# A hybrid GLA / DeltaNet layer: timed VectorE and ScalarE steps kept in emission order, the modulation's last step as a task, other charges on the planner's clock

## The chip, the cores and the metric

One core of a Trainium2 chip. The time is the device time of one launch, in microseconds (us). The engines are TensorE (PE in the profile; PEld its weight loads), VectorE (DVE), ScalarE (ACT), GpSimd (POOL) and SyncE (SP, which issues most DMAs). In the trace each runs its instructions in the order in which the built program lists them.

## The reference

One layer of a streaming encoder on 512 prompt and 64 sample tokens, width 2048, in float32:

```python
mod = jax.nn.silu(c) @ w_ada[l] + b_ada[l]
sh1, sc1, g1, sh2, sc2, g2 = jnp.split(mod[:, None, :], N_MOD, axis=-1)
h = rmsnorm(x, norm1[l]) * (1 + sc1) + sh1
mix, s_a, s_b, s_c = token_mixers(h, ...)      # w_in, GLA (4 heads) and gated DeltaNet (8 heads), w_out
x = x + g1 * mix
h = rmsnorm(x, norm2[l]) * (1 + sc2) + sh2
f, s_f = conv_ffn(h, ...)                      # w_up, causal conv of width 3, silu(gate) * val, w_down
x = x + g2 * f
```

A DeltaNet head normalizes q and k, forms two 128x128 matrices of decays for each block, solves a triangular system (the inverse of 1 + lower), and carries a state through the blocks. A GLA head does the like with a decay for each channel. `c` is one vector for the prompt and one for the sample.

## The kernel before

**Stages.** `head` (to about 180 us): norm, the first third of the modulation, and the first projections. Then the mixers (`gdn_heads`, `gla_heads`): projection tiles of `w_in`, each 16 steps of six matmuls (`mm6`: activations and weights are each split into a rounded part `h` and a rest `l`, and three of the four products are taken). Between those steps the work of the heads is woven in. Then the output projection's first half (k = 8 to 15), after it the second half (from about 1140 us), whose activations `oa` are loaded from DRAM and rounded by `load_o`; last the FFN (`up`, `down`), the longest stage.

**Weights.** `wtile`/`split` loads 128x1024 weights into a `raw` buffer (three of them), rounds them on ACT into `wh`, and takes the rest on DVE into `wl`.

**Jobs, tasks, ada.** Every PE step calls `tick`. It moves the planner's clock `now` on by 0.795 us and asks three kinds of Python generators for work: tasks (convolutions, gates), jobs (the heads: `gdn`, `gla`) and `ada`, the last two thirds of the modulation. `ada` adds up on DVE, in 512-column steps, `acc += w * c`; one block of 512 outputs takes 64 such steps (`acc` in the profile), and there are 16 blocks. At a block's end `ada_sum` sums over the partitions with PE (L1095), copies to `rows` on ACT, transposes and adds the bias (`put_mod`).

**The clock.** Every instruction that goes through `_Timed` is charged to its engine by `charge`, from `OP_US`: a base and a price for an element, added to the time at which the engine comes free (`free`), or to the job's own chain. A generator yields (`until`, `hop`, `pause`) until `now` has passed the end of what it waits for; only then is its next instruction emitted. So the clock decides between which projection steps a head's matmuls stand.

**Who orders the queues.** After emission the framework's scheduler lists the instructions. It goes by priority, which is the place of emission, and takes the next one whose producers it holds for ready. `high_priority(offset=80)` moves an instruction 80 places ahead. Weights have that (`split`), and so do all DVE and ACT steps of the jobs (`_Sooner`). `issue_after(x)` puts an instruction behind `x` on its engine.

**The inverse.** In `inverse16` a head's matrix goes to DRAM and comes back as 32 small 16x16 blocks, 28 dependent DVE steps invert them (L432 and L433, `m<-m 32x14` and the like), they go out again and come back as `cm`, and two DVE steps (L449) make of them the tiles that PE reads at L263.

In the profile all timed steps have the lines of their helpers: L2248 for `_Timed`, L2224 for the jobs' steps, L2264 for their matmuls, L2260 for transposes, L2278 for POOL. In the changed kernel these are L2272, L2247, L2287, L2283 and L2305.

## Time and profile before

| what | us |
|---|---|
| median of 3 runs (2776.75 to 2779.93) | 2779.32 |
| the profiled execution's own time | 2773.29 |
| its span, first to last instruction | 2771.5 |
| PE busy in the span | 2719.0 |
| DVE busy | 2276.2 |
| ACT busy | 1298.6 |
| POOL busy | 468.7 |

A line of a group reads: line, engine, operation, output <- inputs, shape, count | busy us, mean ns of one | idle time of the engine just before them, and what ended most of it. A line of the waits reads: who waits and at which line, for whom; then us in total, how often, the longest. A line in order of time reads: start, duration, what, and in brackets the idle time before it and its releaser.

### The profile page before, as it was taken

What the parts mean: (1) busy time and instruction counts of PE and PEld (TensorE: products, weight loads), DVE (VectorE), ACT (ScalarE), POOL (GpSimd) and SP (SyncE); (2) the same over time, 40 slices, a digit from 0 to 9 for tenths busy, and PEclk for the clock granted to TensorE, in tenths of its full rate; (3) what the DMA queues carried; (4) which work ended last, traced back from release to release, by engine and by line L of the source; (5) the groups of instructions that cost most, each with busy time, mean ns of one, the idle gap of its engine ahead of it and who ended that gap; (6) DMA issues with size and microseconds to landing.
All of it is one profiled execution on the core that took longest, in us unless ns stands there. A gap on an engine that the chain in (4) does not pass through costs nothing.

```text
span 2771.5 us, 52615 instructions
## 1 busy us (share of the span) xinstructions
PE 2719.0 (98%) x20528; PEld 2651.8 (96%) x20528; DVE 2276.2 (82%) x3682; ACT 1298.6 (47%) x2269; POOL 468.7 (17%) x440
## 2 busy tenths in 40 slices
PE   7999999999999999999999999999999999999998
PEld 5799999999999999999999999999999999999998
DVE  4578787877878887678999999999999976888896
ACT  4255555464544442355454545444444445333453
POOL 0001000010000000000333333333333300000141
PEclk9999999999999999999999999999999999999999
DMA  9985545555545667634555555554646496764752
GB/s 310 339 263 166 139 137 146 148 148 141 172 139 143 178 180 224 179 101 120 152 166 159 173 153 178 153 181 144 182 142 190 139 315 181 223 209 129 238 175 86
DMA packets 647198, 487.59 MB, mean 176 GB/s; under 512 B 66953, under 2 KB 569988, under 8 KB 646948
## 3 DMA queue, kind: packets, MB, share of 16 engines
q1 hardware_dynamic: 633844, 470.74, 56.7%
q10 hardware_dynamic: 13104, 13.47, 1.7%
q8 instruction: 162, 2.65, 0.4%
q14 instruction: 88, 0.72, 0.1%
HBM read 400.08 MB, written 84.04 MB: 175 GB/s over the span
## 4 chain that ended last, share of the span: by engine, by line
PE 81%; DVE 10%; DMA 3%; issue 2%; ACT 2%; POOL 1%; SPq 0%; ACTq 0%; DVEq 0%; POOLq 0%
PE g L651 16%; PE bank L1738 16%; PE bank L1737 16%; PE bank L1739 16%; PE g L653 8%; PE bank L2264 4%; DVE acc L2248 2%; DVE wl L1647 2%; PE bank L651 1%; PE bank L2260 1%; DVE wl L2248 1%; PE bank L878 1%; DVE m L2224 1%; DVE slot L1933 1%; PE bank L653 1%
## 5 line engine op out<-in xcount | busy, mean ns | idle before, releaser
L1738 PE MATMUL bank<-slot,wh 128*128 128x290 f32 (+1 forms) x3584 | 1067.3, 298 | 0.0
L1737 PE MATMUL bank<-slot,wh 128*128 128x290 f32 (+1 forms) x3584 | 1063.2, 297 | 1.1 <-DVE v L1760 0.6
L1739 PE MATMUL bank<-slot,wl 128*128 128x290 f32 (+1 forms) x3584 | 1059.9, 296 | 0.7 <-DVE wl L1647 0.6
L1739 PEld LDWEIGHTS bank<-slot,wl 128*128 128x128 f32 x3584 | 680.0, 190 | 2.3 <-DVE wl L1647 1.9
L1737 PEld LDWEIGHTS bank<-slot,wh 128*128 128x128 f32 x3584 | 675.1, 188 | 5.7 <-issue 4.4
L1738 PEld LDWEIGHTS bank<-slot,wh 128*128 128x128 f32 x3584 | 677.0, 189 | 0.1
L651 PE MATMUL g<-hh,wh 128*128 128x288 f32 x2048 | 469.9, 310 | 0.6 <-ACT wh L1044 0.3
L653 PE MATMUL g<-hh,wl 128*128 128x288 f32 x2048 | 441.6, 296 | 2.9 <-DVE wl L1046 2.3
L1645 ACT ACTIVATE wh<-raw 128x1024 fp32r<-128x1024 f32 (+1 forms) x304 | 280.6, 923 | 347.8 <-PE bank L1738 322.7
L651 PE MATMUL g<-hl,wh 128*128 128x288 f32 x2048 | 442.2, 297 | 0.3 <-DVE hl L682 0.2
L1647 DVE TENSOR_TENSOR wl<-raw,wh 128x1024 fp32r<-128x1024 f32 (+1 forms) x304 | 372.3, 1225 | 69.7 <-ACT wh L1645 67.5
L1645 ACT ACTIVATE wh<-s 128x1024 fp32r<-128x1024 f32 (+1 forms) x228 | 210.9, 927 | 297.4 <-PE bank L1738 138.0
L651 PEld LDWEIGHTS g<-hh,wh 128*128 128x128 f32 x2048 | 324.8, 189 | 16.2 <-issue 10.5
L653 PEld LDWEIGHTS g<-hh,wl 128*128 128x128 f32 x2048 | 330.3, 189 | 5.1 <-DVE wl L1046 2.7
L651 PEld LDWEIGHTS g<-hl,wh 128*128 128x128 f32 x2048 | 330.1, 189 | 3.3 <-issue 2.3
L1647 DVE TENSOR_TENSOR wl<-s,wh 128x1024 fp32r<-128x1024 f32 (+1 forms) x228 | 251.1, 1103 | 14.5 <-ACT wh L1645 13.4
L2248 ACT ACTIVATE wh<-raw 128x1024 fp32r<-128x1024 f32 x135 | 142.8, 1058 | 192.4 <-PE g L651 176.5
L2248 DVE TENSOR_TENSOR wl<-raw,wh 128x1024 fp32r<-128x1024 f32 x135 | 165.7, 1228 | 50.0 <-ACT wh L2248 47.3
L2248 DVE SCALAR_TENSOR_TENSOR acc<-aw,ct,acc 128x512 f32<-128x512 f32 x284 | 201.7, 744 | 1.5 <-DMA aw<-in_w_ada_dram 1.4
L1861 POOL TENSOR_TENSOR j<-j,j 128x288 f32<-128x288 f32 (+1 forms) x120 | 186.1, 1558 | 83.8 <-ACT j L1865 82.1
L2248 DVE SCALAR_TENSOR_TENSOR acc<-xr,ct,acc 128x512 f32<-128x512 f32 x196 | 141.1, 748 | 0.3 <-DVE rq L2224 0.3
L1933 DVE TENSOR_TENSOR slot<-bank,slot 128x288 f32<-128x288 f32 x184 | 83.2, 452 | 33.6 <-PE bank L1739 32.1
(330 smaller groups left out, 3309.3 us busy)
## 6 DMA issues: line engine op xcount, KB each, us to landing
raw<-in_w_up_dram SPq DMA_DIRECT2D x176, 512.0 KB
raw<-in_w_in_dram SPq DMA_DIRECT2D x100, 512.0 KB
raw<-in_w_down_dram SPq DMA_DIRECT2D x128, 320.0 KB
aw<-in_w_ada_dram SPq DMA_DIRECT2D x79, 512.0 KB
slot<-cd SPq DMA_DIRECT2D x140, 288.0 KB
cd<-j SPq DMA_DIRECT2D x120, 288.0 KB
xr<-in_w_ada_dram SPq DMA_DIRECT2D x49, 512.0 KB
hraw<-in_w_ada_dram SPq DMA_DIRECT2D x40, 512.0 KB
```

Source lines behind the costliest of these rows:

```text
L651: T.matmul(ps[:, h if bank is None else bank, :n], wh, x[:, h, :n], start=f, stop=False)
L653: T.matmul(ps[:, h if bank is None else bank, :n], wl, ah[:, h, :n], start=False, stop=stop)
L878: T.matmul(ps[32 * k:32 * k + 32, :w], cs[:, k0 + k], got[n][k // per][:, k % per], start=(n == together - 1 + 8 * g + 4 * (1 - mi)), stop ...
L1645: self.nc.scalar.activation(hi, src, AF.Copy)
L1647: self.nc.vector.tensor_tensor(lo, src, hi.bitcast(F32), op=ALU.subtract)
L1737: T.matmul(ps, wh[:, j], hi, start=(c < 3 and j == 0), stop=False, skip_group_check=True)
L1738: T.matmul(ps, wh[:, j], lo, start=False, stop=False, skip_group_check=True)
L1739: T.matmul(ps, wl[:, j], hi, start=False, stop=(j == n - 1), skip_group_check=True)
L1861: minus = lambda out, a, b: G.tensor_tensor(out, a, b, op=ALU.subtract)
L1933: V.tensor_tensor(dst, ps, dst, op=ALU.add)
L2248: return f(*a, **kw)
L2264: return self.engine.matmul(out, *a, **kw)
```

## The change

It has four parts.

1. `_Timed` keeps, for DVE and for ACT, the last timed instruction and emits the next one with `issue_after` on it. So all timed steps of an engine stand in emission order, the jobs' too. The weight roundings of `split` are exempt (`floating`).
2. `ada_sum` no longer waits for the copy to `rows`: the copy, the transposes and the bias become a task (`ada_put`), and `ada` goes on with its next block. A second `drain` at the stage's end takes what such a task may leave.
3. ACT's charges: 0.09 us and 1/1060 us for an element in place of 0.10 and 1/960; 0.06 instead of 0.2 where a sum is accumulated; 0.06 for a bias or scale by columns; 1.28 where the function's table differs from the last one's (exp, silu, ln). The 2.6 us charged by hand in `gla_gate` go. DVE's steps with a sum lose their 0.2.
4. POOL's power for the norms is charged 1.0 us more than its base in place of 0.7.

```diff
-OP_US = {"V": (0.12, 1 / 960.0), "A": (0.10, 1 / 960.0), "G": (0.45, 1 / 400.0)}
+OP_US = {"V": (0.12, 1 / 960.0), "A": (0.09, 1 / 1060.0), "G": (0.45, 1 / 400.0)}
+TABLE_US, COLUMN_US = 1.28, 0.06
+TABLES = {AF.Exp: "exp", AF.Silu: "silu", AF.Ln: "ln"}
...
-        self.slower("G", 0.7)
+        self.slower("G", 1.0)
...
+    def action(self, func, *a, **kw):
+
+        us = 0.06 if "accum_out" in kw else 0.0
+        if any(isinstance(kw.get(n), bass.AP) for n in ("bias", "scale")):
+            us += COLUMN_US
+        table = TABLES.get(func, self.table)
+        if table != self.table:
+            self.table, us = table, us + TABLE_US
+        return us
+
+    def behind(self, key):
+
+        last = self.last_of.get(key)
+        return nullcontext() if self.floating or last is None else self.tc.issue_after(last)
...
             nc.sync.dma_start(raw[:, :n_].rearrange("p (k n) -> p k n", k=k), src)
+            self.floating = True
             self.ta.activation(hi[:, :n_], raw[:, :n_], AF.Copy)
             self.tv.tensor_tensor(lo[:, :n_], raw[:, :n_], hi[:, :n_].bitcast(F32), op=ALU.subtract)
+            self.floating = False
...
+        self.spawn(self.ada_put(blk, ps))
+
+    def ada_put(self, blk, ps):
         rows = self.sp.tile([P, 256], F32, tag="qc", bufs=3, name=self.name("rows"))
-        _, at = self.timed(self.ta.activation, rows, ps[:, :256], AF.Copy)
-        yield from self.pause(at)
+        self.ta.activation(rows, ps[:, :256], AF.Copy)
+        yield from self.until()
...
                 yield from self.pause(self.free["V"] + HOP_US)
-                yield from self.ada_sum(blk, acc)
+                self.ada_sum(blk, acc)
...
-        self.slower("A", 2.6)
...
-            self.k.charge(self.key, _size(out), 0.2 if "accum_out" in kw else 0.0)
-            return f(*a, **kw)
+            self.k.charge(self.key, _size(out), self.k.action(*a[2:], **kw) if name == "activation" else 0.0)
+            with self.k.behind(self.key):
+                r = f(*a, **kw)
+            if not self.k.floating and self.key in "VA":
+                self.k.last_of[self.key] = self.k.tc.nc.cur_bb.bb.instructions[-1]
+            return r
```

No instruction is added or removed on DVE or PE; four of ACT's table loads go. From the end of `head` to the end of the first half of the output projection nearly every queue is in another order; before and after that they are the same but for a few rows.

**DVE, the inverse of head 6** (the seventh). `acc` is the modulation's sum, `wl` a weight's rest, `mod` the bias of a block; `sq` and `st` belong to another head's state. Before, from its first step:

```order
L2224 MEMSET m_6380 32x16
L2224 TENSOR_TENSOR m_6380<-m_6380 32x14
L2248 TENSOR_SCALAR acc_7390<-aw_7131,ct 128x512
L2224 TENSOR_TENSOR m_6380<-m_6380 32x14
L2248 SCALAR_TENSOR_TENSOR acc_7389<-aw_7131,ct,acc_7389 128x512
L2224 TENSOR_TENSOR m_6380<-m_6380 32x13x2
L2248 SCALAR_TENSOR_TENSOR acc_7390<-aw_7131,ct,acc_7390 128x512
L2224 TENSOR_TENSOR m_6380<-m_6380 32x13x2
L1066 TENSOR_TENSOR mod<-bank_7382,cols 128x4
L2224 TENSOR_TENSOR m_6380<-m_6380 32x12x3
```

and after:

```order
L2247 MEMSET m_6335 32x16
L2247 TENSOR_TENSOR m_6335<-m_6335 32x14 x2
L2247 TENSOR_TENSOR m_6335<-m_6335 32x13x2 x2
L2247 TENSOR_TENSOR m_6335<-m_6335 32x12x3 x2
L2247 TENSOR_TENSOR m_6335<-m_6335 32x11x4 x2
L2247 TENSOR_TENSOR m_6335<-m_6335 32x10x5 x2
L2247 TENSOR_TENSOR m_6335<-m_6335 32x9x6 x2
L2247 TENSOR_TENSOR m_6335<-m_6335 32x8x7 x2
L2247 TENSOR_TENSOR m_6335<-m_6335 32x7x8 x2
L2247 SCALAR_TENSOR_TENSOR st_7327<-st_7249,egl,bank_7325 128x128
L2272 SCALAR_TENSOR_TENSOR acc_6688<-aw_7043,ct,acc_6688 128x512
```

Between the first step and the copy that ends the chain stood 36 other instructions; now there are 5 (two `acc`, one each of `st`, `sq`, `wl`).

**ACT, while head 2 carries its state and head 4 begins.** `ncum` and `cum` are head 4's decays (of the row `m_4782`, loaded from `gd`), `sq` is the copy in head 2's state that PE waits for, `qkv` a convolution's silu. Before:

```order
L2224 ACTIVATE m_5084<-m_4782,ncum 128x128 x2
L2248 ACTIVATE conv_in<-g_4557 128x512
L2224 ACTIVATE sq_4773<-bank_4771 128x128
L2248 ACTIVATE wh_4990<-raw_4989 128x1024
L2224 ACTIVATE m_4025<-bank_4801,rq_3906 128x128
L2248 ACTIVATE ca_4777<-conv_in,cols 128x579
```

and after, with head 2's last copy and head 4's key:

```order
L2272 ACTIVATE conv_in<-g_4770 128x512
L2272 ACTIVATE ca_4964<-conv_in,cols 128x579
L2247 ACTIVATE sq_5041<-bank_5039 128x128
L2247 ACTIVATE m_4061<-bank_5053,rq_3870 128x128
L2272 ACTIVATE wh_5257<-raw_5256 128x1024
L2272 ACTIVATE qkv_4963<-ca_4964 128x512
L2272 ACTIVATE ts_5093<-ca_4964 128x64
L2247 ACTIVATE scrap,s_729_5109<-m_4061 128x128
```

The decays stood ahead of the copy; now they come only after these rows, behind the silu of their own key.

**ACT, the end of the first half of the output projection.** `rows` is the copy of the last modulation block, the slots are the roundings of the second half's activations (`oa`), `wh` weights. Before:

```order
L2248 ACTIVATE wh_13341<-raw_13340 128x1024
L2248 ACTIVATE rows_13326<-bank_13321 128x256
L1475 ACTIVATE slot_13416<-xr_13414 128x576
L1475 ACTIVATE slot_13422<-raw_13420 128x576
L1475 ACTIVATE slot_13428<-xr_13426 128x576
L1475 ACTIVATE slot_13434<-raw_13432 128x576
```

and after:

```order
L2272 ACTIVATE wh_13226<-raw_13225 128x1024
L2272 ACTIVATE rows_13146<-bank_13141 128x256
L1497 ACTIVATE slot_13416<-xr_13414 128x576
L2272 ACTIVATE wh_13286<-raw_13285 128x1024
L1497 ACTIVATE slot_13422<-raw_13420 128x576
L1497 ACTIVATE slot_13428<-xr_13426 128x576
L1497 ACTIVATE slot_13440<-xr_13438 128x576
L1497 ACTIVATE slot_13434<-raw_13432 128x576
L2272 ACTIVATE wh_13346<-raw_13345 128x1024
```

The last block's copy came after all of the first half's weights; now weights of its last two tiles (`wh_13286`, `wh_13346`) are rounded behind it, between the slots. On PE the matmuls that it waits for (L1095) stood 56 matmuls ahead of the second half's first one, and now 200.

## The prediction

> **What bounds the kernel now.** I read the page first, then the stages, then PE's waits in the stage that the change touches, then the queue that ended each long wait.

> ```profile
> span 2771.5 us, 52615 instructions
> PE 2719.0 (98%) x20528; PEld 2651.8 (96%) x20528; DVE 2276.2 (82%) x3682; ACT 1298.6 (47%) x2269; POOL 468.7 (17%) x440
> ...
> 180.00:1147.00 967.00, 948.80 (x7283) 921.11 (x7282) 784.00 (x1652) 464.45 (x1048) 64.63 (x71) 1.00 0.57 161
> 1147.00:2771.50 1624.50, 1611.08 (x11993) 1604.28 (x11992) 1394.08 (x1803) 767.37 (x1091) 398.71 (x352) 1.00 0.56 170
> ```

> The two stretches are rows of the view by windows: length, then busy time and count of PE, its weight loads, DVE, ACT and POOL, then the granted clock (1.00 in both), the DMA share and GB/s. PE is the bound. The timed steps lie in the middle stretch (180 to 1147 us, mixers and the first half of the output projection): there PE is busy 948.8 of 967 us, so an order of DVE and ACT can win back at most some 18 us, 0.66% of the span. The count of instructions on PE does not change. So the whole question is who makes PE wait there:

> ```profile
> PE bank L2264 <- DVE m L2248: 5.4, 3, 2.6
> PE g L651 <- ACT wh L2248: 3.8, 1, 3.8
> PE bank L2260 <- ACT qkv L2248: 2.5, 2, 1.5
> PE bank L2264 <- ACT sq L2224: 2.4, 2, 1.9
> PE bank L2264 <- DVE st L2224: 1.5, 2, 0.9
> PE bank L2264 <- DVE m L2224: 1.3, 2, 0.6
> PE g L653 <- DVE wl L2248: 1.1, 2, 0.7
> PE bank L1737 <- DVE v L1760: 0.6, 1, 0.6
> PE bank L1739 <- DVE wl L1647: 0.2, 1, 0.2
> PE bank L2264 <- DVE sq L2224: 0.2, 1, 0.2
> ```

> These are PE's waits from 180 to 1300 us: total, times, longest. L1737 and L1739 belong to the FFN, which is not touched; the others sum to 18.2 us. That is the stock from which the change can take.

> **The chains of small steps (5.4 us).** The 16-row inverse of each head is a chain of 28 small DVE steps; its result comes back by DMA as `cm`, becomes the two tiles `m` (L2248 here), and PE waits for these. For head 6 of nine, counted from 0: two groups of DVE from 614.5 us on, the chain's own window (DVE alone), the pieces that follow on the critical chain, and PE's wait; below the dots head 4, its window and one stretch of its DVE:

> ```profile
> L2248 DVE SCALAR_TENSOR_TENSOR acc<-xr,ct,acc 128x512 f32<-128x512 f32 x8 | 5.9, 735 | 0.0
> L2224 DVE TENSOR_TENSOR m<-m 32x14 f32<-32x14 f32 (+6 forms) x28 | 5.6, 199 | 0.0
> 614.50:637.70 23.20, 22.41 (x68) 1.00 0.60 172
> 637.73 3.76 DMA d<-m
> 641.50 1.94 DMA cm<-d
> 644.82 0.43 PE L2264 MATMUL bank<-m,m 128*128 128x64 f32 x2 [2.59 <-DVE m L2248]
> ...
> 475.50:484.90 9.40, 8.53 (x36) 1.00 0.25 65
> 476.80 2.93 DVE L2224 TENSOR_TENSOR m<-m 32x26 f32<-32x26 f32 x13
> ```

> In head 6 the 28 steps take 23.2 us though they are only 5.6 us of work, because after nearly each of them stands another instruction, above all the modulation's `acc` steps; 36 others stand inside. In head 4 the chain takes 9.4 us and 13 steps in a row cost 2.93 us, 225 ns each. The new order puts 5 others inside head 6's chain (quoted with the change): 28 x 0.225 = 6.3, two `acc` at 0.735, one `wl` of about 1.2, two small ones: some 10 us. That is 13 us earlier against a wait of 2.6. The planner now emits the chain and its consumer from this shorter sum too, so not all 13 us become slack, but the two transfers (3.76 + 1.94 = 5.7) stand against a charge of 3.1 + 3.6 = 6.7. I take the 5.4 us to zero; bounds 5.4 (the waits stay) and 0. Late next, where the chain is not: the `m` evictions of L2224.

> **The end of the stage (4.2 us).**

> ```profile
> 1132.51 0.64 PE L1095 MATMUL bank<-acc,consts 128*32 128x256 f32 x8
> 1133.22 0.39 ACT L2248 ACTIVATE rows<-bank 128x256 f32<-128x256 f32 x1 [11.77 <-PE bank L1095]
> 1133.50 0.68 ACT L1475 ACTIVATE slot<-xr 128x576 fp32r<-128x576 f32 x1
> 1143.50 1.06 ACT L2248 ACTIVATE wh<-raw 128x1024 fp32r<-128x1024 f32 x1 [1.12 <-DMA raw<-in_w_out_dram]
> 1144.61 0.86 PE L651 MATMUL g<-slot,wh 128*128 128x288 f32 x4 [3.84 <-ACT wh L2248]
> 1145.87 0.85 PE L653 MATMUL g<-slot,wl 128*128 128x288 f32 x2 [0.40 <-DVE wl L2248]
> ```

> ACT stands 11.77 us before `rows`, the last modulation block's copy, which needs the matmuls of L1095 at 1132.51. The eight roundings of the second half's activations (L1475) queue behind it; they hold the `raw` buffers, so the next weight is loaded late and PE waits 3.84 + 0.40. Now the modulation does not stop for each of its 16 copies. Counted in the two orders, 56 matmuls lie between the last L1095 and the second half's first matmul before, 200 now. 144 of them at 0.13 us (948.8 us for 7283 in the stretch's row) are 19 us earlier. The roundings can then run while the weights of the first half are still used, and the load has over 10 us in hand. Minus 4.2; bounds 4.2 and 0.

> The price of not stopping: the next block's first `acc` step overwrites the sum that L1095 reads, and DVE waits for PE at its head. Such steps wait already (row below: 4.1 us over 31); twice that, 8 us of DVE, is hidden in the 183 us that DVE idles in this stretch (967 - 784).

> **ACT held by steps that ran ahead (4.9 us).**

> ```profile
> L2248 DVE TENSOR_SCALAR acc<-aw,ct 128x512 f32<-128x512 f32 x31 | 14.4, 494 | 4.5 <-PE bank L1095 4.1
> L2224 ACT ACTIVATE m<-m,ncum 128x128 f32<-128x128 f32 x36 | 12.6, 391 | 10.8 <-DMA m<-gd 10.8
> 398.16 0.69 ACT L2224 ACTIVATE m<-m,ncum 128x128 f32<-128x128 f32 x2 [1.90 <-DMA m<-gd]
> 399.24 0.26 ACT L2224 ACTIVATE sq<-bank 128x128 f32<-128x128 f32 x1
> 223.55 1.28 ACT L2248 ACT_TABLE_LOAD   x1
> 224.84 0.63 ACT L2248 ACTIVATE qkv<-ca 128x512 f32<-128x512 f32 x1
> L2224 DVE TENSOR_SCALAR rq<-rq 128x4 f32<-128x4 f32 x9 | 1.5, 171 | 8.1 <-POOL rq L2278 8.1
> ```

> A job's decay steps (`ncum`) are hoisted before their row has landed, and ACT stands 10.8 us for it; at 398.16 the copy `sq`, which PE needs, stood behind (1.9 of the 2.4). In the new order the decays stand behind their own head's silu, some 16 steps of projection after the load is issued. The silu `qkv` at 224.84 came behind two exponentials and a table load that the clock charged at nothing; PE waited 1.47. Now the table is charged 1.28 and the silu stands first. Minus 2.5 and minus 2.4; bounds 4.9 and 0. DVE is likewise held 8.1 us at nine `rq` steps that wait for POOL, and the `st` copies behind them cost PE 1.5; POOL is now charged 0.45 + 0.01 + 1.0 = 1.46, so `rq` is emitted later. I take 1.0 of 1.5.

> [...] The load starts at 223.55, takes 1.28, and the silu starts at 224.84, 0.01 after it. [...]

> **What stays, and what is new.** I leave the `m` and `sq` waits of L2224 (1.5), the other `wl` (0.7) and 0.5 of `st`: 2.7. New waits come from what the clock still has wrong:

> ```profile
> L2224 ACT ACTIVATE scrap<-bank 128x128 f32<-128x128 f32 x72 | 20.4, 283 | 21.1 <-PE bank L2260 20.1 <-ACT scrap L2224 0.2
> L2224 ACT ACTIVATION_READ_ACCUMULATOR scrap<-bank 128x1 f32 x72 | 14.9, 207 | 0.0
> L2278 POOL TENSOR_TENSOR s<-s,mhalf 128x4 f32<-128x4 f32 (+1 forms) x18 | 20.9, 1161 | 409.3 <-DVE s L2248 409.3
> ```

> A step that sums its squares is now charged 0.09 + 128/1060 + 0.06 = 0.27 (0.43 before); the rows give 0.283 and up to 0.283 + 0.207 = 0.49. Four of them before the output's normalization are up to 0.9 us late, for nine heads 7.9 us: upper bound; 0 is the lower, since POOL's charge is 0.3 over its row (1.46 against 1.16) on the same path. I take 2.0, near the lower. Kept out of strict order, weight roundings stay where they are: nothing.

> Sum: -5.4 - 4.2 - 4.9 - 1.0 + 2.0 = -13.5 us. The profiled span becomes 2758.0; its run took 2773.29, so 2759.8; that run lies 6.0 under the median of 2779.32, so I predict 2765.8.

> **Rivals.**
> 1. *The end stays as it is* (the load is late for another reason, such as the four w_up loads now ahead of it on SP): 4.2 us come back, 2770.0. For it: DMA was busy 0.57 of this stage. Against: over 10 us in hand.
> 2. *The waits are only moved.* The planner places PE's steps as tightly as its clock allows; each head's state takes four blocks with three hops through an eviction, 108 in nine heads, placed as close as the clock lets them. If each is 0.1 us late, 10.8 come back: 2776.6, no change. For it: shorter chains make the planner place consumers sooner. Against: PE's rows above show that waits came from queues held by a DMA, by POOL or by others' steps, and not at the many equally tight places.
> 3. *Slower: DVE held by late transfers.* In strict order everything on DVE stands behind a step whose transfer is late; there are two such steps in each of nine chains, 18.

> ```profile
> 785.71 4.09 DMA cm<-d
> L2248 DVE TENSOR_TENSOR m<-cm,consts 128x512 f32<-128x512 f32 x18 | 11.8, 688 | 2.3 <-DMA cm<-d 2.3
> ```

> One such transfer took 4.09 against 3.6 charged. It decides from (15.5 + 5.6) / 18 = 1.2 us of PE per place; at 1.25 it gives 15.5 - 22.5 = +7.0: 2786.3. Against: today those steps hold DVE 2.3 us in all.
> 4. *A table switch holds ACT for longer than the load*, say as long again (1.28): at the nine key transposes that follow a silu 11.5 come back, 2777.3. [...] *The order does not change what PE sees*: 2779.3. The quoted rows of the load and of the chains speak against both.

> **How the numbers follow.** About 0.2% (5.6 us) is what a measurement here can tell from none. Forecast 0.66, rival 1 0.09: faster 0.75. Rival 2 0.12, rival 4 0.04: same 0.16. Rival 3: slower 0.09. Low end: all 18.2 go and nothing comes, 2761.1, less 2 for runs that spread over 3.2: 2759. High end: through rival 2 to 2778, which leaves out rival 3 and most of rival 4.

> **What would show it.** Right: PE's waits of 180 to 1300 us fall from 19.0 to about 5.5; no wait of PE for the two tiles `m` (L2272 there); each chain of 28 steps in 9 to 12 us; ACT does not stand before the last `rows`, and no wait of 3.8 us opens the second half; DMA `m<-gd` and POOL `rq` no longer end idle time on ACT and DVE. FFN and head as before. Wrong: new waits of 0.3 to 1 us at the `sq`, `st` and `m` evictions (rival 2), or DVE idle before `m<-cm` in tens of us (rival 3).

## The result, and the profile after

The changed kernel takes 2754.11 us (median of 5 runs, 2751.71 to 2754.93), the kernel before beside it 2778.68 us (5 runs, 2776.02 to 2779.93): a ratio of 0.9912, interval 0.9898 to 0.9927. That is 24.6 us, or 0.88%. The forecast was faster, by 13.5 us to 2765.8; the measured time lies below its range, and the gain is 1.8 times the one forecast. Repeated later (`e8_after_again`), the gain was 19.8 us, 1.5 times the forecast. One run of the kernel before in a later comparison took 3272.55 us at a mean granted clock of 0.752; it is left out of every figure below.

The page of the changed kernel, then the view by windows for the two stretches that the prediction quotes: 180 us to the start of the second half of the output projection, and from there to the end (columns as there).

```profile
span 2752.4 us, 52667 instructions
PE 2713.4 (99%) x20528; PEld 2647.8 (96%) x20528; DVE 2282.9 (83%) x3682; ACT 1292.6 (47%) x2265; POOL 468.2 (17%) x440
...
180.00:1127.50 947.50, 945.75 (x7293) 919.16 (x7292) 791.39 (x1661) 459.13 (x1047) 66.47 (x71) 1.00 0.60 168
1127.50:2752.40 1624.90, 1611.28 (x12002) 1604.83 (x12000) 1395.59 (x1804) 769.05 (x1092) 396.40 (x352) 1.00 0.55 168
```

The second stretch is as long as before (1624.5, now 1624.9). The whole gain lies in the first: 967.0 has become 947.5. PE idled 18.2 us there and now idles 1.75 (947.50 - 945.75). PE's waits from 180 to 1300 us, after:

```profile
PE bank L2291 <- ACT m L2247: 0.7, 1, 0.7
PE bank L1759 <- DVE v L1782: 0.6, 1, 0.6
PE bank L2291 <- DVE st L2247: 0.3, 1, 0.3
PE bank L2291 <- DVE m L2272: 0.3, 1, 0.3
PE bank L2291 <- DVE sq L2247: 0.3, 1, 0.3
PE bank L1761 <- DVE wl L1669: 0.2, 1, 0.2
PE g L669 <- ACT hh L1497: 0.2, 1, 0.2
```

They sum to 2.6 us where they were 19.0, so 16.4 us of waiting are gone. But the page's own busy time of PE has fallen too, from 2719.0 to 2713.4, for the same 20528 matmuls. Waits do not explain that. The view by windows of the kernel *before*, cut at three of its waits (2.22, 1.86 and 3.84 us), shows what does; the third figure from the end of a row is PE's granted clock (then the DMA share and GB/s).

```profile
257.70:261.10 3.40, 1.18 (x11) 0.95 (x9) 3.36 (x7) 0.00 (x0) 0.00 (x0) 1.00 0.96 254
261.10:264.50 3.40, 3.40 (x18) 3.40 (x18) 1.75 (x4) 2.19 (x7) 0.00 (x0) 0.50 0.36 127
264.50:267.90 3.40, 3.40 (x31) 3.40 (x30) 3.11 (x7) 0.83 (x4) 0.00 (x0) 0.99 0.11 10
397.70:401.10 3.40, 1.55 (x12) 1.55 (x13) 1.31 (x4) 2.94 (x7) 0.00 (x0) 1.00 0.29 80
401.10:404.50 3.40, 3.40 (x16) 3.40 (x15) 3.02 (x6) 3.38 (x10) 0.00 (x0) 0.50 0.46 123
1141.80:1145.20 3.40, 0.59 (x4) 0.56 (x4) 1.90 (x4) 1.64 (x2) 0.00 (x0) 1.00 1.18 299
1145.20:1148.60 3.40, 3.00 (x13) 2.73 (x12) 1.84 (x2) 1.06 (x1) 0.00 (x0) 0.50 1.20 292
```

After the waits at 258, 398 and 1141 us, PE counts as busy again but runs at half its clock for 3.4 us. The row from 261.1 to 264.5 counts 18 matmuls, the next one 31. At a clock of 0.50 each such stretch costs up to half its length, 1.7 us, which no row of waits shows: three of them are up to 5.1 us. In the changed kernel no such stretch lies between 180 us and PE's last matmul. This is the term that the prediction lacks.

In the profiled executions, 2771.5 becomes 2752.4: -16.4 (waits) - 5.1 (half clock) = -21.5. The head of the program, which is not touched, took 2.6 us more in this execution of the changed kernel (19 fewer matmuls by 180 us, x1238 against x1257; the 1257th starts at 182.53 instead of 179.97): loads landed later, as in the row below (7.5 before). That makes -18.9 of the measured -19.1. In the second profile of the changed kernel (`e8_after_again`) the head again had x1257, and the span was 2750.3.

```profile
PE g L829 <- DMA consts<-in_consts_dram: 8.9, 1, 8.9
```

### The profile page after: what moved, and what is told of

Its sections match the earlier page's. It is cut to its first block, busy times and chain, and to the rows that moved or that the text cites. A ratio compares the mean times of both kernels' runs of the same rounds, so it can differ in the third digit from the quotient of the medians.

```text
span 2752.4 us, 52667 instructions
## 1 busy us (share of the span) xinstructions
PE 2713.4 (99%) x20528; PEld 2647.8 (96%) x20528; DVE 2282.9 (83%) x3682; ACT 1292.6 (47%) x2265; POOL 468.2 (17%) x440
## 4 chain that ended last, share of the span: by engine, by line
PE 89%; DVE 6%; DMA 3%; issue 1%; ACT 0%; SPq 0%; POOL 0%; ACTq 0%; DVEq 0%
PE g L669 21%; PE bank L1760 16%; PE bank L1759 16%; PE bank L1761 16%; PE g L671 10%; PE bank L2291 5%; DVE wl L1669 2%; PE bank L2287 1%; PE bank L669 1%; DMA hraw<-in_w_ada_dram 1%; PE bank L898 1%; DMA raw<-in_w_down_dram 1%; DVE slot L1955 1%; PE bank L671 1%; DVE m L2247 1%
## 5 line engine op out<-in xcount | busy, mean ns | idle before, releaser
L1760 PE MATMUL bank<-slot,wh 128*128 128x290 f32 (+1 forms) x3584 | 1067.3, 298 | 0.0
L1760 PEld LDWEIGHTS bank<-slot,wh 128*128 128x128 f32 x3584 | 677.0, 189 | 0.1
L1669 DVE TENSOR_TENSOR wl<-s,wh 128x1024 fp32r<-128x1024 f32 (+1 forms) x228 | 251.3, 1104 | 13.6 <-ACT wh L1667 12.5
L2272 ACT ACTIVATE wh<-raw 128x1024 fp32r<-128x1024 f32 x135 | 143.4, 1062 | 183.8 <-PE g L669 159.0
L2272 DVE SCALAR_TENSOR_TENSOR acc<-aw,ct,acc 128x512 f32<-128x512 f32 x280 | 198.8, 745 | 3.6 <-DMA aw<-in_w_ada_dram 3.5
L2272 DVE TENSOR_TENSOR wl<-raw,wh 128x1024 fp32r<-128x1024 f32 x135 | 166.3, 1232 | 21.4 <-ACT wh L2272 20.5
L2272 DVE SCALAR_TENSOR_TENSOR acc<-xr,ct,acc 128x512 f32<-128x512 f32 x200 | 142.8, 746 | 0.0
```

The source lines that it names most:

```text
L1669: self.nc.vector.tensor_tensor(lo, src, hi.bitcast(F32), op=ALU.subtract)
L1760: T.matmul(ps, wh[:, j], lo, start=False, stop=False, skip_group_check=True)
L2272: r = f(*a, **kw)
```

## The experiments

Each comparison ran on one chip, beside runs of the kernel before on that chip. The kernel before took 2773.1 to 2774.8 there (median of each comparison), so differences are taken within a comparison. `before` and `after` stand for the two kernels; edits are shown against `after` unless said otherwise.

### The parts alone

The change has three parts: the emission order (`behind`), the last step of the modulation as a task (`ada_put`), and the new charges of the clock. Each was run alone, by undoing the other two.

`e1_order_only`: charges and last step as before.

```diff
-OP_US = {..., "A": (0.09, 1 / 1060.0), ...}
+OP_US = {..., "A": (0.10, 1 / 960.0), ...}        # and the other charges
-                self.ada_sum(blk, acc)
+                yield from self.ada_sum(blk, acc)   # rows copied there, with a pause
```

> The kernel before with the emission order alone (weight roundings free), the old charges and the old last step of the modulation. Theory A (the order carries the chains on VectorE and the blocked copies on ScalarE, and every wait of PE of about 2 us or more brings a stretch of 3.4 us at half clock, worth 1.7 us): the nine chains have 0 to 9 other operations inside instead of 4 to 36, so the waits for DVE m (5.4) and ACT sq (2.4) go and two of the three half-clock stretches with them (3.4); the end wait (4.2) and its half-clock stretch stay, since 56 matmuls stand there as before. 2779 - 5.4 - 2.4 - 3.4 - 1 = about 2767 us. Rival B (the nearer clock does the work, the order only freezes what the clock got wrong): 2776 to 2786 us, with new waits for steps held behind late ones.

Measured: 2762.86 against 2773.81, ratio 0.9964 (0.9952 to 0.9977), 11.0 us faster. PE's longest wait, with what ACT did before it:

```profile
PE g L669 <- ACT wh L2269: 6.2, 2, 4.0
PE bank L2284 <- ACT qkv L2269: 0.9, 1, 0.9
...
1121.75 0.38 ACT L2269 ACTIVATE rows<-bank 128x256 f32<-128x256 f32 x1 [11.77 <-PE bank L1115]
1133.30 1.33 PE L669 MATMUL g<-slot,wh 128*128 128x288 f32 x4 [4.00 <-ACT wh L2269]
```

Of the waits for `m`, `sq`, `st` and `qkv` only 1.2 us are left, although the charges are the old ones. The end wait stays (4.0 of the 6.2 us; the other 2.2 lie at 1019 us), with ACT standing 11.77 us before `rows` exactly as before. Theory A holds; rival B falls.

`e2_put_only`: the task alone.

```diff
     def behind(self, key):
-        last = self.last_of.get(key)
-        return nullcontext() if ... else self.tc.issue_after(last)
+        return nullcontext()                        # and the old charges
```

> The kernel before with the last step of the modulation as a task alone. The last sum then stands 242 matmuls ahead of the second half of the output projection instead of 56. Theory A: the wait for wh and wl at 1144 us (4.2) and its half-clock stretch (1.7) go, the chains stay (2, 10, 19, 4, 16, 15, 32, 31 and 20 others inside, five of them 16 or more where there were three): 2779 - 5.9 = about 2773 us, up to 4 us more for the two added long chains. Rival B (the wait at 1144 us has another cause, the loads): 2779 us, the wait still there.

Measured: 2766.14 against 2773.81, ratio 0.9974 (0.9965 to 0.9983), 7.7 us faster. The wait for `wh` at the second half is gone, and so is the half clock behind it; 12.3 us of other waits outside the feed-forward stay, of which the largest is `qkv` with 4.1. As theory A has it, with 2 us more than expected.

`e3_clock_only`: the new charges alone (`behind` as in e2, the last step as in e1), against `before`:

```diff
-OP_US = {..., "A": (0.10, 1 / 960.0), ...}
+OP_US = {..., "A": (0.09, 1 / 1060.0), ...}
+TABLE_US, COLUMN_US = 1.28, 0.06
...
-        self.slower("G", 0.7)
+        self.slower("G", 1.0)
...
-        self.slower("A", 2.6)
...
```

> The kernel before with the new charges alone (ScalarE's price, column, table switch, 1.0 on GpSimd). Theory A: the chains keep 5 to 37 others inside (five above 16, three before), and the last sum stands only 2 matmuls ahead of the second half of the projection instead of 56, so the end wait grows by 54 x 0.133 = 7 us; ScalarE's qkv waits (2.5) go: 2779 + 7 + 2 to 5 - 2.5 = about 2787 us. Rival B (the nearer clock does the work): 2765 us or less.

Measured: 2782.05 against 2773.81, ratio 1.0030 (1.0019 to 1.0041), 8.2 us *slower*.

```profile
PE g L668 <- ACT wh L2267: 10.4, 1, 10.4
PE bank L1114 <- DVE acc L2267: 4.6, 1, 4.6
```

The new charges by themselves move the last sum of the modulation to 2 matmuls ahead of the second half, and the end wait grows from 3.8 to 10.4 us, with 20.5 us at half clock around it. ACT stands 24.72 us before the last `rows` there, although nothing keeps it in emission order. Theory A expected 8 us slower; rival B (that the nearer clock does the work) falls.

`e4_before_again`: the kernel before, unchanged, for a second profile.

> The kernel before once more, for a second profile. Its first profiled execution took 2773.3 us, its timed runs 2776.0 to 2779.9. Theory A (waits of PE bring stretches of 3.413 us at half clock on a grid that runs free of the program, so the same wait brings one in some executions and none in others): the same waits to within 1 us, and 4 to 6 half-clock stretches between 180 and 1300 us where the first profile has 3, for 2775 to 2780 us. Rival B (the loads land otherwise in each execution): 3 such stretches, and waits that differ by 3 us or more.

Measured: 2772.35, with 16.1 us of waits from 180 to 1300 us (19.0 in the first profile) and four half-clock stretches (two in a row at 261.7 and two at 1142.3; none at 401, where the wait for `sq` was 1.5 instead of 1.9 us). So waits vary by 3 us between executions, which theory A had put within 1 us, and the number of stretches varies beside them, which rival B had put at three. Neither theory had the time right: 2772 is what the kernel before takes in these comparisons. Why it took 2776 to 2780 beside the first measurement is not settled; those runs left no trace.

### The parts taken out one by one

`e5_no_order`, `e6_no_put` and `e7_no_clock` each undo one part of `after`; `e8_after_again` is `after`.

```diff
     # e5: behind()
-        return nullcontext() if self.floating or last is None else self.tc.issue_after(last)
+        return nullcontext()
     # e6: ada_sum() and ada_put() in one again
-        self.ta.activation(rows, ps[:, :256], AF.Copy)
-        yield from self.until()
+        _, at = self.timed(self.ta.activation, rows, ps[:, :256], AF.Copy)
+        yield from self.pause(at)
...
     # e7: the old charges (OP_US, 0.7 for POOL and the 2.6 us by hand as before, too)
-            self.k.charge(..., self.k.action(*a[2:], **kw) if name == "activation" else 0.0)
+            self.k.charge(..., 0.2 if "accum_out" in kw else 0.0)
```

> The changed kernel without the emission order (the task and the new charges stay). Theory A (order, task and charges each have a place of their own): the task took 7.7 us alone, the chains have 36, 21, 19, 18 and 28 others inside again, so waits for DVE m and ACT sq of 5 to 9 us with one to three half-clock stretches (1.7 each) come back: 8 to 14 us faster than before. Rival C (the charges and the task together place the steps, the order adds little): 20 to 25 us faster, like the whole change.

Measured: 2765.35 against 2773.06, ratio 0.9977 (0.9964 to 0.9989), 7.7 us faster. The nine chains, each from the first to the end of the last of its 28 steps, take 8 to 22 us again, 120.2 in all (123.9 before, 81.5 in the changed kernel), and PE waits at the tiles that hang on them:

```profile
PE bank L2290 <- DVE m L2246: 4.0, 4, 1.3
PE bank L2290 <- DVE m L2271: 2.7, 2, 1.4
PE bank L2290 <- DVE sl L2246: 2.3, 2, 1.8
```

That is just under theory A's 8 to 14 us. Rival C falls.

> The changed kernel with the old last step of the modulation (order and new charges stay). The last sum stands 2 matmuls ahead of the second half of the output projection. Theory A: the wait of 10 us for wh at that place comes back as with the charges alone (10.4 us, and 20.5 us at half clock, worth 10.2), on top of the whole change: 24.6 - 10.4 - 5 to 10 = 4 to 9 us faster than before. Rival C (the order alone keeps ScalarE's roundings ahead, the task adds little): 18 us faster or more.

Measured: 2771.21 against 2773.06, ratio 0.9990 (0.9981 to 0.9999), 1.9 us faster. Two rows of the timeline and one window:

```profile
1128.08 0.38 ACT L2268 ACTIVATE rows<-bank 128x256 f32<-128x256 f32 x1 [22.72 <-PE bank L1115]
1138.39 1.33 PE L669 MATMUL g<-slot,wh 128*128 128x288 f32 x4 [9.36 <-ACT wh L2268]
...
1128.70:1142.30 13.60, 4.24 (x17) 3.64 (x17) 8.29 (x12) 6.78 (x10) 0.00 (x0) 0.50 0.89 236
```

ACT stands 22.72 us before the last `rows`, PE waits 9.36 us at the second half, and for 13.6 us around it the clock is halved. The roundings behind the copy start only after it, as in `e3_clock_only`. There ACT stood 24.72 us without the emission order, so the order is not what makes the hold; both kernels have the new charges and the old last step, and in both the last sum stands 2 matmuls ahead of the second half. With the old charges the old last step cost less: `e1_order_only` waits 4.0 us there. So the new charges pay only together with the task, and rival C falls. The measured gain lies under the 4 to 9 of theory A; the place and the size of the wait are as it said.

> The changed kernel with the old charges (order and task stay). Theory A: the order alone took 11.0 and left the end wait of 6.2 us and 6.8 us at half clock (3.4); the task takes both: 20 to 21 us faster than before, so that the charges are worth 4 us in the whole. Rival C (the order only works on a near clock): 12 us faster or less, with waits of 0.5 to 2 us at the heads' blocks.

Measured: 2754.30 against 2773.06, ratio 0.9928 (0.9916 to 0.9940), 18.8 us faster, a little under theory A's 20 to 21 and far from rival C's 12. PE's waits are gone with the old charges as well:

```profile
PE bank L1760 <- DVE v L1783: 0.6, 1, 0.6
PE bank L2292 <- DVE st L2248: 0.6, 1, 0.6
PE bank L2292 <- DVE sl L2248: 0.5, 1, 0.5
PE bank L2292 <- DVE sq L2248: 0.2, 1, 0.2
PE bank L2292 <- DVE m L2273: 0.2, 1, 0.2
```

> The changed kernel once more beside the three, on the same chip: 22 to 26 us faster than before, no half-clock stretch between 180 and 1300 us, and under 4 us of waits there.

Measured: 2753.30 against 2773.06, ratio 0.9924 (0.9912 to 0.9936), 19.8 us faster, a little under the expected 22 to 26; no half-clock stretch from 180 us to the end of the work, and 1.7 us of waits. With e7 beside it, the new charges are worth 1.0 us in the whole change, which the two intervals do not tell from nothing; theory A had 4. Order and task add up: 11.0 + 7.7 = 18.7 against 18.8 for both.

### The order, engine by engine

`e9_order_dve` keeps the order on VectorE alone, `e10_order_act` on ScalarE alone:

```diff
     def behind(self, key):
-        return nullcontext() if self.floating or last is None else ...
+        return nullcontext() if self.floating or last is None or key != "V" else ...   # e10: "A"
```

> The changed kernel with the emission order on VectorE alone (ScalarE's timed steps go where the scheduler puts them). Theory A (most of the order's 12 us are the nine chains on VectorE): the chains have 2 to 8 others inside as in the whole change, waits under 3 us remain between 180 and 1300 us, among them ACT qkv or sq: 2754 to 2757 us. Rival D (the order pays on ScalarE, where hoisted decay steps block the copies): 2760 to 2765 us, with waits for ACT sq and qkv of 4 us and more.

Measured: 2760.36 against 2774.82, ratio 0.9945 (0.9931 to 0.9958), 14.5 us faster. The chains are short (84.0 us in all), but the time misses theory A's 2757 by 3 us, and 7 us of waits are left where it had under 3. Rival D, which has the time, has the wrong place: no wait for ACT `sq` or `qkv` is left. (The kernel before took 1.8 us more here than in the comparison of e8, so both theories' times are uncertain by as much.) The longest wait left is one near 1034 us, with two stretches at half clock (6.8 us) around it:

```profile
PE bank L2291 <- DVE sl L2247: 2.6, 1, 2.6
PE g L669 <- ACT wh L2272: 1.1, 1, 1.1
...
1033.63 0.48 DVE L2247 SCALAR_TENSOR_TENSOR sl<-sl,s,bank 128x256 f32<-128x256 f32 x1 [4.47 <-DMA out_dram<-sl]
```

DVE stands 4.47 us there for a store of the tile that it is to write. Why that store is late without ScalarE's order was not tried.

> The changed kernel with the emission order on ScalarE alone. Theory A: the chains on VectorE have 14, 36, 8, 21, 5, 15, 6, 18 and 29 others inside, nearly as without any order (9, 36, 12, 21, 6, 19, 6, 18, 28), so the waits for DVE m, sl and st (9.7 us there) stay: 2762 to 2767 us. Rival D: 2754 to 2757 us.

Measured: 2763.02 against 2774.82, ratio 0.9958 (0.9945 to 0.9971), 11.8 us faster, inside theory A's 2762 to 2767; the chains take 122.7 us in all, and the waits for `m` are back:

```profile
PE bank L2291 <- DVE m L2272: 3.8, 2, 2.1
PE bank L2291 <- DVE m L2247: 2.1, 2, 1.1
```

From no order (7.7 us faster), VectorE's adds 6.8 and ScalarE's 4.1; both together 12.1. VectorE's comes out the larger, as theory A has it, but the intervals of e9 and e10 overlap, so which is larger is not shown; ScalarE's is not small.

### What a wait costs beyond its length

Two kernels put 19 waits of PE into the first part of the feed-forward of `after`, where it has hardly any. The output is unchanged.

```diff
         if c == 0:
             self.p1 = tmp("p1")
-            A.activation(self.p1, x, AF.Copy)
+            if t in range(5, 43, 2):
+                zero, w = self.zero3[:, :1], self.a[t, "w", 1][0][:, 0, :1]
+                with self.tc.high_priority(offset=80):
+                    for _ in range(1):                               # e12: range(3)
+                        A.activation(self.p1, x, AF.Copy)
+                    A.activation(zero, self.p1[:, :1], AF.Copy, scale=0.0)
+                    A.activation(w, w.bitcast(F32), AF.Identity, bias=zero)
+            else:
+                A.activation(self.p1, x, AF.Copy)
```

> The changed kernel with 19 waits of PE put into the first part of the feed-forward, where it has none: at every second unit the weights of the next product are written once more, after a copy of the product just made and a small step (about 0.39 + 0.2 + 0.2 us on ScalarE and what stands between; estimate 1.2 to 1.8 us of waiting each, 23 to 34 in all). The output is unchanged. Theory A (a wait brings a stretch at half clock only where PE idles some 1.9 us or more of one 3.413 us window): 0 to 4 such stretches, so the time is 2753 plus the waits plus 0 to 7 us. Rival E (each wait brings a stretch, or none does): 19 stretches, 32 us beside the waits, or none.

> The same with two more copies and a longer step ahead of the write (estimate 2.6 to 3.4 us of waiting each, 50 to 65 in all). Theory A: more than 15 of the 19 waits bring a stretch of 3.4 us at half clock, worth 1.7 us each, so the time is 2753 plus the waits plus 26 to 40 us. Rival F (a wait costs its own length): 2753 plus the waits, 2803 to 2818 us.

Measured: 2797.47 for the short waits and 2861.95 for the long ones, where `after` takes 2753.30. First PE's waits that the edit brings (short, then long; in the long kernel the weights' rest `wl` comes late as well, so that each of its 19 places has two), then two windows of the short-waits kernel, two of the long-waits one, and last the window of 1300 to 2300 us in `e8_after_again`, in the short and in the long:

```profile
PE bank L1759 <- ACT p L1775: 25.0, 19, 1.3
PE bank L1759 <- ACT wh L1777: 4.7, 19, 0.3
...
PE bank L1759 <- ACT p L1775: 42.1, 19, 2.2
PE bank L1761 <- DVE wl L1669: 22.5, 19, 1.3
...
1487.60:1491.00 3.40, 2.09 (x17) 1.85 (x15) 3.35 (x5) 2.47 (x4) 0.00 (x0) 1.00 0.63 170
1491.00:1494.40 3.40, 3.15 (x21) 2.92 (x22) 2.66 (x3) 1.23 (x3) 1.75 (x2) 1.00 0.52 162
...
1347.40:1350.80 3.40, 0.54 (x2) 0.30 (x2) 3.40 (x5) 2.58 (x5) 0.59 (x1) 1.00 0.80 230
1350.80:1354.20 3.40, 2.93 (x12) 2.93 (x13) 0.42 (x1) 0.48 (x3) 3.32 (x5) 0.50 0.54 163
...
1300.00:2300.00 1000.00, 999.51 (x7408) 995.39 (x7407) 896.34 (x1014) 492.04 (x637) 330.12 (x287) 1.00 0.58 176
1300.00:2300.00 1000.00, 969.26 (x7069) 955.89 (x7068) 846.82 (x971) 480.89 (x634) 298.85 (x284) 0.99 0.55 166
1300.00:2300.00 1000.00, 935.38 (x6599) 922.21 (x6598) 790.48 (x904) 463.70 (x627) 288.42 (x275) 0.96 0.49 146
```

A matmul takes 999.51 / 7408 = 0.135 us there. The long waits lose 809 matmuls in these 1000 us, 109 us, of which PE idles 64.6; the other 44.5 are lost while PE counts as busy. The trace has 26 windows of 3.413 us at half clock there, at least one behind each of the 19 waits (seven have two), 88.7 us in all: 44.4 us if PE worked through all of them, 4.4 less for the 8.9 us that it idles inside. Rival F, under which a wait costs its own length, would give 2818; it falls. Theory A's top is 2753 + 64.6 + 40 = 2858, 4 us short, of which 1.8 may be this comparison's.

The short waits lose 339 matmuls, 45.8 us, of which PE idles 30.7. Three of 19 bring a half-clock stretch (5.1 us); that is theory A's 0 to 4, and against rival E. But 10 us remain, 0.5 us for each wait, so the time is 7 us above theory A's top (2753 + 29.7 + 7 = 2790). The trace shows that remainder behind each wait: there the starts of PE's matmuls lie 1.61, 0.24, 0.54 and 0.24 us apart, where 0.135 is usual. That is 2.1 us lost, of which the rows of waits count 1.6. Why the later starts are late too was not tried.

## Why the prediction was right and wrong

**Right: where the gain lies, and who makes PE wait.** The stretch to 1147 us carries the whole gain. The chains do what the prediction says. Head 6's window, then the group of its 28 steps and the others inside, after:

```profile
599.90:608.70 8.80, 8.54 (x66) 8.30 (x65) 7.97 (x35) 2.19 (x4) 0.00 (x0) 1.00 0.32 78
...
L2247 DVE TENSOR_TENSOR m<-m 32x14 f32<-32x14 f32 (+6 forms) x28 | 5.3, 188 | 0.8
L2272 DVE SCALAR_TENSOR_TENSOR acc<-aw,ct,acc 128x512 f32<-128x512 f32 x2 | 1.5, 730 | 0.0
```

It takes 8.8 us where it took 23.2, and 10 were forecast; all nine take 6.9 to 10.9. The wait for the two tiles `m` is 0.3 us (5.4 before). e5, e9 and e10 show that VectorE's order is what shortens them.

**Right in size, wrong in one sign: the end of the stage.** The end wait is gone, and e2 and e6 show that the task is what takes it away: with the task alone it is gone, and without the task 9.4 us are there. But the forecast that ACT would no longer stand before the last `rows` is wrong. It stands 5.38 us; the row comes 26.5 us ahead of the second half (1127.59), so nothing hangs on it.

```profile
1101.06 0.39 ACT L2272 ACTIVATE rows<-bank 128x256 f32<-128x256 f32 x1 [5.38 <-PE bank L1115]
```

**Right in size, the cause in part wrong: ScalarE's 4.9 us.** The waits for `qkv` and `sq` are gone, and ACT stands 1.7 us for the decay rows where it stood 10.8; DVE stands 0.3 at `rq` where it stood 8.1. The prediction gave the `qkv` part to the table switch that is now charged, and the `rq` part to POOL's higher charge. For `rq` the order does it: DVE stands 0.7 us there with the order alone (e1) and nothing in e7, without POOL's charge, but 8.0 with the charges alone (e3) and 7.5 in e5. For PE's waits for `qkv` and ACT's `sq` the order is enough, without the new charges: e1 has 0.9 of `qkv` left, e7 nothing. But it is not the only way: e5, with the task and the charges and without the order, has no `qkv` wait and 0.6 of `sq`. So what each part does to these two is open. The charges alone make the kernel slower (e3).

```profile
L2247 ACT ACTIVATE m<-m,ncum 128x128 f32<-128x128 f32 x36 | 14.0, 389 | 1.7 <-DMA m<-gd 1.7
L2247 DVE TENSOR_SCALAR rq<-rq 128x4 f32<-128x4 f32 x9 | 1.5, 164 | 0.3 <-POOL rq L2305 0.3
L2272 DVE TENSOR_SCALAR acc<-aw,ct 128x512 f32<-128x512 f32 x32 | 14.1, 483 | 10.5 <-PE bank L1115 9.5 <-DMA aw<-in_w_ada_dram 0.8
```

The price of the task, DVE's wait for PE at the head of the next block, is 9.5 us over 32 steps (4.1 over 31 before), and it is hidden, as forecast: 8 us had been put for it.

**Wrong: what stays and what is new (2.9 us).** The prediction left 2.7 us of old waits and 2.0 of new ones beside the feed-forward's 0.8; 2.6 are there in all. No wait for the sums of squares appeared, whose 2.0 had been taken near the lower of two bounds. The lower was the right one.

**Wrong: the time of a matmul was taken as fixed (5.1 us).** The step that failed is "win back at most some 18 us". It reads a wait's price from the rows of waits, and the granted clock from a row over 967 us. There the half-clock stretches, 8.6 us of 967 (the third one ends behind the row), disappear in rounding: the row says 1.00. A window of 3.4 us behind the wait says 0.50. The stretch became 19.5 us shorter, more than the 18 that were called its most. e12 shows the price by itself: 64.6 us of waits cost 109.

**Wrong: the step from the profiled run to the median (6.0 us).** The profiled run of `before` lay 6.0 under the median, and the prediction put the same 6.0 on the changed kernel. There it is nothing: its profiled run is its median (2754.11). This offset belongs to `before`, not to the measurement. In the later comparisons `before` spreads from 2770.3 to 2779.2, and its time tends to be longer where its mean granted clock is lower: 2770.3 to 2774.8 at 0.997, 2770.8 to 2776.7 at 0.996, 2772.5 to 2776.8 at 0.995, 2779.2 at 0.994; the changed kernel stays within 4 us (2751.1 to 2754.9) at 0.997 to 0.998. The two profiles of `before` have three and four half-clock stretches between 180 us and PE's last matmul. That such stretches were all of the 6.0 is not shown, and its cause stays open. In the later comparison, where the median of `before` is 2773.1, the gain is 19.8 us.

The sum: 2765.8 - 2.9 - 5.1 - 6.0 + 2.6 (the head) = 2754.4, against 2754.1. The low end of the range, 2759, was built as "all waits go" and had the last two faults in it.

**The rivals.** Rival 1 (the load at the end stays late), rival 2 (waits only moved) and rival 3 (DVE held by late transfers) did not come: DVE stands 1.5 us at `m<-cm` in all, 2.3 before. Rival 4 did not come either: no wait of PE for a silu is left, and in `after` the silu `qkv` at 297.40 us starts 0.02 us after the end of its load (296.10 us, 1.28 long). So nothing shows a table switch that holds ACT for longer than its load. The rival's other half, an order that changes nothing for PE, falls with e1.

## What to carry to other kernels

A list scheduler that fills one engine's gaps with whatever is ready can also put long independent steps between short dependent ones, and hoist steps whose data is late; both hide in a busy engine and show only as the other engine's waits. If the program's emission order is already planned, try keeping it. Look also for a step that waits for something far off and holds the steps behind it on its engine: here one copy held ScalarE's roundings with and without the emission order (e6 and e3), and making it a task of its own took that away. And when a wait of TensorE is priced, look at the granted clock in a window of a few microseconds behind it: the wait of 1.86 us brought a half-clock stretch worth up to 1.7 us more.
